# A hybrid decoder layer: twenty of 52 projection blocks as seven half-size products, and the mLSTM and attention steps beside the remaining ones

## The chip, the cores and the metric

One Trainium2 chip, one core. The metric is the device time of one execution in microseconds; lower is better. The kernel before takes 1984.62 us (median of three runs, 1983.13 to 1986.1).

## What is computed

One step of a decoder layer for a prompt of 1024 tokens and a group of 8 x 4 sample tokens that share all weights (1056 columns in all; D = 1024):

```python
h = LN0(x) * (1 + scale1) + shift1
z = h @ w_in + b_in        # mLSTM q, k (4 x 128), v, og (4 x 256), i, f; attention q (16 x 64), k, v (4 x 64); gm, ga (1024)
A = mlstm(q, k, v, i, f, state)              # 4 heads, chunks of 128, running max
B = window_attention(qa, ka, va, cache)      # 16 heads on 4 groups, window 128, sinks, ALiBi
merged = sigmoid(gm) * (A * sigmoid(og) @ w_bm) + sigmoid(ga) * (B @ w_ba)
x = LN1(alpha * x + gate1 * (merged @ w_out))
h2 = LN0(x) * (1 + scale2) + shift2
x = LN2(alpha * x + gate2 * (glu(conv3(h2 @ w_up)) @ w_down))
```

All in fp32; the outputs are both groups' rows and the new states (C, n, m, keys, values, convolution).

## The kernel before

An fp32 product is made of three products of parts: each operand is split into a high part (a cast to the reduced type, ScalarE) and a low part (operand minus high part, VectorE), and TensorE adds hi x hi, hi x lo and lo x hi in PSUM. The core's eight PSUM banks are L (three, for the projections), PD (two), PE, PF and PG (side work).

The projection `h @ w_in` goes in 52 blocks of 128 features and one of gate rows (`gate`, L1197 on). A block runs over three token tiles (384, 384, 288) and 8 chunks of D: 3 x 24 matmuls of `group` (L440 to L451). `evac_in` (L1170 on) takes each tile out of PSUM; ScalarE adds the bias or takes the tanh (L1180, L1184), VectorE scales (L1182). `Stream` (L393 on) loads a block's weights (L403), casts (L424) and subtracts (L428) a block or two ahead.

All else of this stage is *side work*, written as generators: `gate_rows` (L632 on: gates, two scans, exponentials), `mlstm(h)` for four heads (L753 on), `swa_pair` and `swa(g)` (L980 on, four attention groups). While the program is written, `pulse(us)` advances a clock by the products' time and takes a step of the first generator in the queue `sides` at `rate[0]` steps a microsecond:

```python
        if sides:
            clock[1] += us * rate[0]
            while clock[1] >= 1.0:
                clock[1] -= 1.0
                step_side()
```

So the order of every engine's instructions is fixed when the kernel is built; at run time each engine goes through its own list in order, and waits where an operand isn't there. The rates in this stage are 0.442, 0.395 and 0.35 (`RATES`, L34). SP issues nearly all DMAs, in one list. `later(us, fn)` puts an issue so many us of products further on. Before the last block `finish_sides()` takes all steps that are left, with no product between them.

An mLSTM head loads (first step) its decay row E (L757), the scaled query factor qA (L758), both spread over 128 partitions, and the old state C in two halves (L761); the second step makes E and the parts of q (L766 to L785); then a chunk of 128 tokens a step: scores and three transposes into bank PE (L799, L196), smT and the parts of v and of the weighted keys (L804 to L807), the products a step later (L789). At its end come the sample tokens, the new state (`new_state`, L906, L910, stored at L915), a norm and `hs`, transposed (L937), and the output rows go to DRAM (`hD`, L943). v and og of the head are still in SBUF from the projection. An attention step copies scores out of PD (L1142, L1143), adds biases, takes the exponentials (L1122), transposes, multiplies with v (L1092) and normalises; one step of a group also holds the sample tokens (L1039 to L1081).

Of the kernel before, what the change touches and what calls it, by code (L numbers as in the profile page):

```python
# [18 lines left out]
D = 1024  # L19
# [31 lines left out]
# columns of the table of constants  # L51
# [52 lines left out]
def hybrid_step(ctx: ExitStack, tc: tile.TileContext, I, O):  # L104
# [85 lines left out]
    # the rows of c in pieces of 128  # L190
# [7 lines left out]
    # vectors along the features, transposed: 0.. b_in (16 + 36 blocks), 52.. b_ada, 100.. norm_w,  # L198
    # 108.. b_down, 116.. b_up, 160.. conv_b, 204.. conv_w (3 x 44)
# [22 lines left out]
    def ada_load(ca, cb, f0, n=256):  # L222
        """Features f0 .. f0 + n of the factors ca and cb: their weights."""
# [43 lines left out]
    # silu(c), transposed  # L267
# [109 lines left out]
    def h_lo(k, ti, eng):  # L377
# [4 lines left out]
        h_f[k][1] += 1  # L382
        if h_f[k][1] == 3:
            drop(h_f.pop(k)[0])

# [1 line left out]
    class Stream:  # L387
        def __init__(self, specs):
            self.specs = specs
            self.raws, self.parts, self.loaded = {}, {}, 0  # L390

        def load(self, upto):
            while self.loaded <= min(upto, len(self.specs) - 1):  # L393
# [14 lines left out]
        def prep(self, i, later_lo=False):  # L408
            if i >= len(self.specs) or i in self.parts:
                return  # L410
# [43 lines left out]
    # ================= phase A: the combined projection, mLSTM, window attention =================  # L454
# [11 lines left out]
    for h in range(4):  # L466
        blk("k", h, 512 + 128 * h)
        blk("q", h, 128 * h)
        if h == 0:
            order.append(("gate", 0))  # L470
            specs.append(("gate",))
        blk("v", 2 * h, 1024 + 256 * h)
        blk("v", 2 * h + 1, 1024 + 256 * h + 128)
        blk("og", 2 * h, 2056 + 256 * h)
        blk("og", 2 * h + 1, 2056 + 256 * h + 128)
    gates = [("gm", j, 4616 + 128 * j) for j in range(8)] + [("ga", j, 5640 + 128 * j) for j in range(8)]
    gates = deque(gates)

    def add_gates(n):
        for _ in range(n):  # L480
            blk(*gates.popleft())
# [5 lines left out]
    blk("ka", 0, 4104)  # L487
    blk("va", 0, 4360)
    add_qa(0)
    add_gates(3)  # L490
    add_qa(1)
    add_gates(2)
    blk("ka", 1, 4104 + 128)
    blk("va", 1, 4360 + 128)
    add_qa(2)
    add_gates(4)
    add_qa(3)
    add_gates(7)

    # the order of all later products: branches, output product, feed-forward  # L500
# [25 lines left out]
    win = Stream(specs)  # L526

    # the first products take the chunks of h as they come
# [64 lines left out]
    # later constants  # L593
    v2, v3, v4 = slot(name="v2"), slot(name="v3"), slot(name="v4")
    rows(v2, 0, I["b_up"], 0, 44)
    rows(v2, 44, I["conv_b"], 0, 44)
    rows(v3, 0, I["conv_w"], 0, 88)
    rows(v4, 0, I["conv_w"], 88 * 128, 44)
# [7 lines left out]
    def late_consts():  # L606
        transpose(PF[:, 0:88], v2[:88, :128], 88)
# [105 lines left out]
    def cache_load(p):  # L713
        """The cached keys and values of a pair of groups."""
# [21 lines left out]
    def norm_tail(num, den, ecol, n):  # L736
        """The layer norm of num / max(|den|, e): its factor is (var(num) + eps max(|den|, e)^2)^-0.5."""
# [37 lines left out]
        # operands in two parts: q, v with a column of ones, the scores and the weighted keys  # L775
# [68 lines left out]
        # the state after the prompt  # L844
# [6 lines left out]
        # the sample group: all its tokens as one block  # L851
# [145 lines left out]
    def swa(g):  # L997
# [37 lines left out]
        def sample():  # L1035
            """The sample group: its rows are (sequence, head, token)."""
# [158 lines left out]
    def gate_rows_in(i):  # L1195
        """The gates' rows: products with both parts of the weights side by side, then their sum."""
# [47 lines left out]
    for h in range(4):  # L1244
        after["og", 2 * h + 1] = [lambda h=h: mlstm(h)]
    after["og", 7].append(state_n_out)
# [5 lines left out]
    def raw_pieces(src, ti):  # L1252
        """Loads a token tile of eight blocks that wait in DRAM."""
# [10 lines left out]
    def refill(raws, ti):  # L1264
        """Puts a token tile into the operand tiles, whose old contents its products have used."""
# [9 lines left out]
    rate[0] = RATES[0]  # L1275
# [611 lines left out]
```

## Time and profile before

| | |
|---|---|
| median of three runs | 1984.62 us |
| span of the profiled execution | 1981.8 us |
| TensorE busy | 1942.6 us, 98% |
| VectorE busy | 997.7 us, 50% |
| ScalarE busy | 723.3 us, 36% |
| GpSimd (POOL) busy | 308.9 us, 16% |
| mean DMA rate | 95 GB/s |

The profile is of one execution; its own time is known by its span, from the first to the last instruction, and the runs are timed apart. Busy times count the instructions on each engine; a matmul's end is modelled, so the distance from one start to the next says more than its length. "Idle before" names what ended the engine's wait. In the window views PEclk is the granted TensorE clock as a share of full speed.

### The profile page before, as it was taken

Reading aid. Unit: us, or ns where it says so; the run is one execution under the profiler, and the core shown is the slowest. Engines: PE = TensorE matmul, PEld = TensorE weight load, DVE = VectorE, ACT = ScalarE, POOL = GpSimd, SP = SyncE. Lnnn points to the kernel's source line nnn. Section 1 sums busy time; section 2 is a strip of 40 time slices with the busy share of each in tenths; the row PEclk is TensorE's granted clock in tenths of the full one; section 3 lists DMA queues with packets and bytes.
Section 4 is the critical chain, followed back from the end, with each engine's and each line's share of the span. In section 5 each row is a group of like instructions: output and inputs, shape, how many; then the busy total and the mean of one; then the engine's idle time right before and its main releaser. Section 6 shows DMA issues by size and latency. Waiting matters only on the chain. (4 is left out here: it accounts for less than half of the span.)

```text
span 1981.8 us, 31279 instructions
## 1 busy us (share of the span) xinstructions
PE 1942.6 (98%) x12597; PEld 1858.1 (94%) x12597; DVE 997.7 (50%) x2166; ACT 723.3 (36%) x1522; POOL 308.9 (16%) x592
## 2 busy tenths in 40 slices
PE   6999999999999999999999999999999999999996
PEld 4899999999998989999999999999999999999995
DVE  4454444444544535241454455564554554645579
ACT  4534334343546445331312454353131312222331
POOL 2013223231123131200000333100000000000007
PEclk9999999999999999999999999999999999999998
DMA  9151424324220322497524142111212020211533
GB/s 289 47 140 25 140 35 119 84 70 100 69 76 23 112 72 60 136 345 244 159 65 128 54 129 67 36 38 48 60 35 62 28 69 27 63 34 49 194 130 130
DMA packets 214362, 187.86 MB, mean 95 GB/s; under 512 B 8849, under 2 KB 197953, under 8 KB 214185
## 3 DMA queue, kind: packets, MB, share of 16 engines
q1 hardware_dynamic: 213437, 185.26, 31.1%
q8 instruction: 98, 1.61, 0.3%
q10 hardware_dynamic: 780, 0.61, 0.1%
q14 instruction: 47, 0.39, 0.1%
HBM read 150.06 MB, written 37.81 MB: 95 GB/s over the span
## 5 line engine op out<-in xcount | busy, mean ns | idle before, releaser
L450 PE MATMUL L<-hhi,whi 128*128 128x384 f32 (+1 forms) x1600 | 526.4, 329 | 0.1
L450 PE MATMUL L<-hlo,whi 128*128 128x384 f32 (+1 forms) x1600 | 517.0, 323 | 0.0
L450 PE MATMUL L<-hhi,wlo 128*128 128x384 f32 (+1 forms) x1600 | 516.5, 323 | 0.0
L450 PE MATMUL L<-mhi,whi 128*128 128x384 f32 (+1 forms) x1248 | 407.4, 326 | 4.9 <-DVE r L1466 3.0
L450 PE MATMUL L<-mhi,wlo 128*128 128x384 f32 (+1 forms) x1248 | 404.1, 324 | 0.4 <-DVE wlo L428 0.4
L450 PE MATMUL L<-mlo,whi 128*128 128x384 f32 (+1 forms) x1248 | 403.3, 323 | 0.0
L428 DVE TENSOR_TENSOR wlo<-wraw,whi 128x1024 fp32r<-128x1024 f32 (+1 forms) x148 | 174.5, 1180 | 331.3 <-ACT whi L424 330.8
L450 PEld LDWEIGHTS L<-hhi,whi 128*128 128x128 f32 x1600 | 301.5, 188 | 6.6 <-issue 4.8
L450 PEld LDWEIGHTS L<-hlo,whi 128*128 128x128 f32 x1600 | 301.9, 189 | 0.3
L450 PEld LDWEIGHTS L<-hhi,wlo 128*128 128x128 f32 x1600 | 301.4, 188 | 0.0
L450 PEld LDWEIGHTS L<-mhi,whi 128*128 128x128 f32 x1248 | 235.4, 189 | 6.7 <-DVE r L1466 3.3
L450 PEld LDWEIGHTS L<-mhi,wlo 128*128 128x128 f32 x1248 | 234.9, 188 | 1.0 <-DVE wlo L428 1.0
L450 PEld LDWEIGHTS L<-mlo,whi 128*128 128x128 f32 x1248 | 235.3, 189 | 0.1
L1511 ACT ACTIVATE u<-L,vT 128x384 f32<-128x384 f32 (+1 forms) x132 | 71.8, 545 | 378.6 <-PE L L450 378.6
L424 ACT CAST whi<-wraw 128x1024 fp32r<-128x1024 f32 (+1 forms) x148 | 149.2, 1009 | 28.3 <-DMA wraw<-in_w_up 25.3
L450 PE MATMUL L<-ahi,whi 128*128 128x384 f32 (+1 forms) x432 | 139.9, 324 | 0.0
L450 PE MATMUL L<-ahi,wlo 128*128 128x384 f32 (+1 forms) x432 | 139.4, 323 | 0.0
L450 PE MATMUL L<-alo,whi 128*128 128x384 f32 (+1 forms) x432 | 139.3, 323 | 0.0
L1524 DVE SCALAR_TENSOR_TENSOR y<-u,vT,y 128x1023 f32<-128x1023 f32 (+3 forms) x92 | 113.7, 1235 | 2.5
L1534 POOL COPY ucol<-u 128x2 f32<-128x2 f32 x44 | 10.3, 234 | 631.7 <-ACT u L1511 631.7
L1680 DVE TENSOR_TENSOR facc<-L,facc 128x384 f32<-128x384 f32 (+1 forms) x120 | 62.7, 522 | 58.6 <-PE L L450 58.4
L298 POOL TENSOR_SCALAR rstd<-mv 128x1 f32<-128x1 f32 (+1 forms) x36 | 22.0, 611 | 400.6 <-DVE mv L307 377.2
(422 smaller groups left out, 2652.4 us busy)
## 6 DMA issues: line engine op xcount, KB each, us to landing
wraw<-in_w_in SPq DMA_DIRECT2D x52, 512.0 KB
wada<-in_w_ada SPq DMA_DIRECT2D x44, 512.0 KB
wraw<-in_w_up SPq DMA_DIRECT2D x44, 512.0 KB
wraw<-in_w_down SPq DMA_DIRECT2D x24, 384.0 KB
hD<-og SPq DMA_DIRECT2D x8, 528.0 KB
gmD<-gm SPq DMA_DIRECT2D x8, 528.0 KB
haD<-ha SPq DMA_DIRECT2D x8, 528.0 KB
gaD<-ga SPq DMA_DIRECT2D x8, 528.0 KB
```

The lines of the kernel that those rows point to most:

```text
L298: G.tensor_scalar(r[:n], var, eps, None, op0=OP.add)
L424: A.copy(hi[:, :n], t[:, :n])
L428: V.tensor_tensor(lo[:, :n], t[:, :n], hi[:, :n].bitcast(F32), op=OP.subtract)
L450: T.matmul(ps[:, :nt], x[:, c], y[:, t0:t0 + nt], start=i == 0, stop=i == last)
L1511: A.activation(u[:, t0:t0 + n], ps[:, :n], AF.Identity, bias=b)
L1524: V.scalar_tensor_tensor(y[:, f:b], u[:, f - d:b - d], w[i], y[:, f:b], op0=OP.mult, op1=OP.add)
L1534: G.tensor_copy(aux["ucol"][:, c, 0:2], u[:, SEQ - 2:SEQ])
L1680: V.tensor_tensor(fx, ps[:, :nt], fx, op=OP.add)
```

## The change

Blocks gm4 to gm7, v0 to v7 and og0 to og7 (twenty) are now made in ten pairs. For a pair (256 features) h and the weights are cut in halves along D (even and odd chunks), features and tokens (two groups of 2 x 264), and Strassen's scheme in Winograd's form takes seven products of 4 chunks each for eight: per pair and token group 7 x 12 matmuls of 264 columns, 168 for a pair, where two blocks had 144 of 384 and 288 columns. The sums of h are made once (`tprep`), those of the weights for each pair on VectorE (`step`); a product's bank, one of all eight in a ring, is added to earlier ones by VectorE or copied by ScalarE. No side work runs meanwhile.

The order is now: gm0 to gm3 in the old way with `tprep` and the first pair's weights beside them at 0.68 steps a us; the ten pairs; the four overwritten halves of h are loaded again; then `gate` and 28 blocks in the old way, at 0.56 steps a us, with all mLSTM and attention steps beside them. The v and og blocks go to DRAM (`pD`) and are loaded in the first step of `mlstm(h)`, ahead of E, qA and C. `mlstm(h)` is queued after block q h.

```diff
-    for h in range(4):
         blk("k", h, 512 + 128 * h)
         blk("q", h, 128 * h)
-        if h == 0:
-            order.append(("gate", 0))
-            specs.append(("gate",))
-        blk("v", 2 * h, 1024 + 256 * h)
...
+    NG = 4
+    for j in range(NG):
+        blk("gm", j, 4616 + 128 * j)
+
+    PAIRS = [(kind, 2 * j, c0 + 256 * j) for kind, c0, js in (("gm", 4616, range(NG // 2, 4)), ("v", 1024, range(4)),
+                                                              ("og", 2056, range(4))) for j in js]
...
+    order.append(("gate", 0))
+    specs.append(("gate",))
+    add_kq(0)
+    add_fill(1)
+    add_kq(1)
+    add_fill(1)
+    add_kq(2)
+    add_fill(1)
+    add_kq(3)
+    add_kva(0)
     add_qa(0)
...
     def mlstm(h):
-        qT, kT, vT0, vT1, og0, og1 = proj["q", h], proj["k", h], proj["v", 2 * h], proj["v", 2 * h + 1], \
-            proj["og", 2 * h], proj["og", 2 * h + 1]
+        qT, kT = proj["q", h], proj["k", h]
+        vT0, vT1, og0, og1 = (slot(name=k) for k in ("v", "v", "og", "og"))
+        for t, key in ((vT0, ("v", 2 * h)), (vT1, ("v", 2 * h + 1)), (og0, ("og", 2 * h)), (og1, ("og", 2 * h + 1))):
+            S.dma_start(t, pD[key])
         E, qA = slot(name="E"), slot(name="qA")
...
+        def step(self, i):
+            if i == 0:
+                self.sums = [slot(name="fsum") for _ in range(2)]
+                self.sum(1, self.q(1, 0), self.q(1, 1), OP.add)
+                self.sum(3, self.q(0, 0), self.q(1, 0), OP.subtract)
+            elif i == 1:
+                self.sum(2, self.s(1), self.q(0, 0), OP.subtract)
+                self.sum(4, self.q(0, 1), self.s(2), OP.subtract)
+                self.pa = self.parts(self.raw[0])
...
+        def product(self, p, g):
+            ps = ring[0][:, :HT]
+            ring.rotate(-1)
+            for kp in range(4):
+                (wh, wl), (xh, xl) = self.weights(p, kp), operand(p, kp, g)
+                for i, (x, y) in enumerate(((wh, xh), (wh, xl), (wl, xh))):
+                    T.matmul(ps, x, y, start=kp == 0 and i == 0, stop=kp == 3 and i == 2)
...
+            if p == 1:
+                A.copy(u1, ps)
+            elif p == 2:
+                self.put(0, g, 0, ps, u1)
+            elif p == 6:
+                V.tensor_tensor(u2, ps, u1, op=OP.add)
+            elif p == 7:
+                V.tensor_tensor(u3, ps, u2, op=OP.add)
+            elif p == 4:
+                self.put(1, g, 0, ps, u3)
+            elif p == 5:
+                V.tensor_tensor(u5, ps, u2, op=OP.add)
+                self.put(1, g, 1, ps, u3)
+            elif p == 3:
+                self.put(0, g, 1, ps, u5)
...
+    rate[0] = 0.68
+    sides.append(first_pair())
+    for i in range(NG):
+        if i == NG - 2:
+            pairs[0].load()
+        direct(i)
+        if i == NG - 1:
+            finish_sides()
...
+    fast(pairs, at_end)
+    drop(hf[0], hf[2], *t3s, *b12)
+    late_loads()
+    rate[0] = 0.56
+    for i in range(NG, len(order)):
+        direct(i)
```

(`put` is one VectorE operation of 264 columns that adds bank, bias and the other term into the finished block.)

**SP, from the end of one mLSTM head to the loads of the next (head 0 to head 1); vD and ogD are the new DRAM copies.** Before:

```order
58 L915 DMA out_s_C<-C0_98_1289 128x8x128
59 L915 DMA out_s_C<-C0_99_1290 128x8x128
60 L403 DMA wraw_126_2129<-in_w_in 128x8x128
61 L943 DMA hD0_689<-og_88_1109 128x1056
62 L943 DMA hD1_690<-og_92_1206 128x1056
63 L403 DMA wraw_130_2216<-in_w_in 128x8x128
64 L757 DMA E_131_2233<-mD_683 128x1056
65 L758 DMA qA_132_2234<-aD_684 128x1056
66 L761 DMA C0_133_2237<-in_state_mlstm_C 128x8x128
67 L761 DMA C0_134_2238<-in_state_mlstm_C 128x8x128
```

and in the changed kernel:

```order
114 L932 DMA out_s_C<-C0_246_3547 128x8x128
115 L932 DMA out_s_C<-C0_247_3548 128x8x128
116 L772 DMA v_268_4272<-vD2_1921 128x1056
117 L772 DMA v_269_4273<-vD3_1863 128x1056
118 L772 DMA og_270_4274<-ogD2_2789 128x1056
119 L772 DMA og_271_4275<-ogD3_2729 128x1056
120 L774 DMA E_272_4280<-mD_675 128x1056
121 L775 DMA qA_273_4281<-aD_676 128x1056
122 L778 DMA C0_274_4284<-in_state_mlstm_C 128x8x128
123 L778 DMA C0_275_4285<-in_state_mlstm_C 128x8x128
124 L960 DMA hD0_681<-og_242_3537 128x1056
125 L960 DMA hD1_682<-og_243_3538 128x1056
```

The loads of E and qA (L757, L758 before; L774, L775 now) stood behind the old head's output rows and a weight load; now they stand behind both stores of the old head's C, directly, and behind four loads of v and og.

**TensorE, at the last block of the projection.** Before, with the block ahead of it and its own first rows:

```order
4738 L450 MATMUL L1_72<-hhi_55_588,whi_369_8386 128x288
4739 L450 MATMUL L1_72<-hlo_56_589,whi_369_8386 128x288
4740 L450 MATMUL L1_72<-hhi_55_588,wlo_370_8387 128x288
4741 L450 MATMUL L2_73<-hhi_29_262,whi_373_8494 128x384
4742 L450 MATMUL L2_73<-hlo_30_263,whi_373_8494 128x384
4743 L450 MATMUL L2_73<-hhi_29_262,wlo_374_8495 128x384
```

and now (PD takes scores, PG and PE transposes, PF the products with v; in place of the dots more of the same kinds):

```order
4899 L447 MATMUL L1_72<-hhi_55_588,wlo_437_8527 128x288
4900 L1154 MATMUL PD0_74<-khi_443_8687,q2_445_8706 128x256
...
4908 L196 MATMUL PG_78<-cst_83,ss_8786 128x128
4909 L196 MATMUL PG_78<-cst_83,ss_8786 32x128
4910 L196 MATMUL PE_76<-cst_83,scr_450_8753 128x128 x4
4911 L1154 MATMUL PD0_74<-khi_443_8687,q2_445_8706 128x256
...
4919 L1090 MATMUL PG_78<-pnT_8928,vs1_7888 64x64 x2
...
4980 L1109 MATMUL PF_77<-scr_454_8757,vn_410_7887 64x256
4981 L447 MATMUL L2_73<-hhi_29_262,whi_440_8678 128x384
4982 L447 MATMUL L2_73<-hlo_30_263,whi_440_8678 128x384
```

Before, one block follows on the other. Now 81 rows of attention (4900 to 4980, twelve steps of the last group) stand between them with no product of a block among them.

## Rows read from the trace of the kernel before

**Rows 1.** The page: busy us of an engine (share of the span) xinstructions.

```profile
PE 1942.6 (98%) x12597; PEld 1858.1 (94%) x12597; DVE 997.7 (50%) x2166; ACT 723.3 (36%) x1522; POOL 308.9 (16%) x592
```

**Rows 2.** Waits of PE in the whole run: us in total, times, longest us.

```profile
PE PE L196 <- DMA v<-in_b_down: 4.9, 1, 4.9
```

**Rows 3.** Window 60 to 760: us, busy us by engine, PEclk, DMA share, GB/s.

```profile
60.00:760.00 700.00, 699.87 (x4719) 665.13 (x4717) 328.22 (x1012) 312.24 (x800) 163.00 (x300) 1.00 0.30 80
```

**Rows 4.** Timeline of PE: start us, us, operation; tiles of 288 and 384 columns.

```profile
910.12 0.29 PE L450 MATMUL L<-hhi,whi 128*128 128x288 f32 x1
...
913.29 0.34 PE L450 MATMUL L<-hhi,whi 128*128 128x384 f32 x1
913.47 0.34 PE L450 MATMUL L<-hlo,whi 128*128 128x384 f32 x1
```

**Rows 5.** The same, an mLSTM product of 258 columns.

```profile
329.06 0.28 PE L789 MATMUL PD<-CTh,qh 128*128 128x258 f32 x1
329.18 0.29 PE L789 MATMUL PD<-CTl,qh 128*128 128x258 f32 x1
```

**Rows 6.** Groups by line and shape, VectorE: busy us, mean ns, idle before.

```profile
L428 DVE TENSOR_TENSOR wlo<-wraw,whi 128x1024 fp32r<-128x1024 f32 x124 | 151.6, 1223 | 278.1 <-ACT whi L424 277.6 <-DMA wraw<-in_w_in 0.5
...
L1271 DVE TENSOR_TENSOR hlo<-raw,hhi 128x384 fp32r<-128x384 f32 x32 | 15.3, 551 | 0.1
```

**Rows 7.** Timelines of PE, DVE and ACT, the start of head 1.

```profile
224.38 1.65 DVE L766 TENSOR_SCALAR E<-E,colQ 128x128 f32<-128x128 f32 x8
...
227.53 1.03 ACT L777 CAST qh<-qA 128x1024 fp32r<-128x1024 f32 x1
...
231.39 0.37 ACT L807 ACTIVATE wx<-PE,colQ 128x128 fp32r<-128x128 f32 x1
...
229.98 0.38 PE L799 MATMUL PE<-q,k 128*128 128x128 f32 x2
```

**Rows 8.** Timelines of PE and ACT, the gates' chain.

```profile
80.54 1.96 PE L1210 MATMUL L<-gpart,cst 32*36 32x384 f32 x6
...
108.90 1.08 ACT L694 ACTIVATE gr<-gr 4x1056 f32<-4x1056 f32 x1
...
110.07 0.74 PE L196 MATMUL PD<-cst,gr 128*128 128x128 f32 x5
```

**Rows 9.** Timeline of SP's DMA queue: issue us, us; heads 0 and 1.

```profile
112.35 9.43 SPq L403 DMA_DIRECT2D wraw<-in_w_in  x2
...
209.75 1.40 SPq L757 DMA_DIRECT2D E<-mD  x1
```

**Rows 10.** Window in which those transfers run (columns as rows 3).

```profile
212.00:216.00 4.00, 4.00 (x25) 4.00 (x24) 1.33 (x2) 0.58 (x1) 0.00 (x0) 1.00 1.07 337
```

**Rows 11.** Timelines of PE and DVE, the end of head 0.

```profile
201.04 0.73 PE L906 MATMUL PD<-wskM,wv 96*128 96x512 f32 x2
...
201.58 2.16 DVE L910 SCALAR_TENSOR_TENSOR C<-C,decb,PD 128x128 f32<-128x128 f32 x8 [2.05 <-PE PD L906]
...
207.24 0.31 PE L196 MATMUL PG<-cst,hs 32*128 32x32 f32 x2
```

**Rows 12.** Timeline of ACT, the copies of three attention steps.

```profile
682.37 0.85 ACT L1142 COPY scr<-PD 128x256 f32<-128x256 f32 x2 [0.57 <-PE PD L1137]
...
688.96 0.62 ACT L1142 COPY scr<-PD 128x256 f32<-128x256 f32 x2
...
692.06 0.61 ACT L1142 COPY scr<-PD 128x256 f32<-128x256 f32 x2
```

**Rows 13.** Windows behind 16 narrow matmuls at 511.36 (columns as rows 3).

```profile
513.00:514.00 1.00, 1.00 (x5) 0.97 (x5) 0.97 (x9) 0.27 (x1) 0.00 (x0) 0.61 1.04 313
514.00:516.00 2.00, 2.00 (x8) 2.00 (x8) 0.08 (x1) 0.43 (x1) 0.00 (x0) 0.50 0.03 8
```

**Rows 14.** Windows in the start (columns as rows 3).

```profile
14.00:20.00 6.00, 1.17 (x6) 0.47 (x4) 2.85 (x6) 1.81 (x2) 1.58 (x6) 1.00 1.06 353
20.00:26.00 6.00, 5.62 (x31) 2.29 (x30) 0.00 (x0) 1.90 (x2) 0.68 (x2) 1.00 1.10 348
```

More of the change, by code (lines that the diff above doesn't have):

```diff
@@ L464, in blk, with add_fill, add_kq @@
         specs.append(spec_in(c0))
[L466 removed]
+    NG = 4
[3 more added lines that the diff above has]
+                                                              ("og", 2056, range(4))) for j in js]
+    fill = deque(range(8))
+    def add_fill(n):
+        for _ in range(n):
+            j = fill.popleft()
+            blk("ga", j, 5640 + 128 * j)
+    def add_kq(h):
         blk("k", h, 512 + 128 * h)
         blk("q", h, 128 * h)
[L469 to L481 removed]
     def add_qa(g):
@@ new lines, in t1_split, with operand @@
+    def t1_split():
+        for kp in range(4):
+            hi, lo = (quarters(t)[:, :, 1, :] for t in acts[2 * kp])
+            x = quarters(hf[2 * kp])[:, :, 0, :]
+            A.copy(hi, x)
+            V.tensor_tensor(lo, x, hi.bitcast(F32), op=OP.subtract)
+        drop(hf[4], hf[6])
+    def operand(p, kp, g):
+        e, o = 2 * kp, 2 * kp + 1
+        if p in (1, 2, 3, 5):
+            k, half_ = {1: (e, 0), 2: (o, 0), 3: (o, 1), 5: (e, 1)}[p]
+            return tuple(quarters(t)[:, g, half_, :] for t in acts[k])
+        if p == 7:
+            return tuple(t[:, g, :] for t in t3_ops[kp])
+        return tuple(quarters(t)[:, g, 0 if p == 4 else 1, :] for t in t_ops[kp])
@@ new lines, in fast @@
+    def fast(pairs, at_end):
+        prev = None
+        t1_split()
+        for n, pr in enumerate([*pairs, None]):
+            nxt = pairs[n + 1] if n + 1 < len(pairs) else None
+            for pos, p in enumerate((1, 3, 6, 2, 7, 4, 5)):
+                who = prev if p == 3 else pr
+                if who is not None:
+                    for g in range(2):
+                        who.product(p, g)
+                if p == 3 and prev is not None:
+                    drop(*prev.ps[1])
+                if pr is None:
+                    if pos == 1:
+                        return
+                    continue
+                if pos == 0:
+                    if n:
+                        pr.step(2)
+                elif pos == 1:
+                    pr.step(3)
+                    pr.step(4)
+                elif pos == 2 and nxt is not None:
+                    nxt.load()
+                elif pos == 3:
+                    drop(*pr.pa)
+                elif pos == 4 and nxt is not None:
+                    nxt.step(0)
+                elif pos == 5:
+                    drop(pr.pq)
+                    if nxt is not None:
+                        nxt.step(1)
+                elif pos == 6:
+                    drop(*pr.ps[0])
+                if nxt is None:
+                    at_end(pos)
+            prev = pr
@@ new lines, in hybrid_step, with finisher, finish, out @@
+    pD = {}
+    def finisher(kind, idx):
+        def finish(blk_, z):
+            j = idx + blk_
+            if kind != "v":
+                A.activation(z, z, AF.Tanh, scale=0.5)
+                f = hnw[:, j:j + 1] if kind == "og" else 0.5
+                V.tensor_scalar(z, z, f, f, op0=OP.mult, op1=OP.add)
+            t = dram.tile([128, TOK], F32, name=f"{kind}D{j}")
+            (gD if kind == "gm" else pD)[kind, j] = t
+            def out():
+                S.dma_start(t, z)
+                drop(z)
+            later(2.0, out)
+        return finish
@@ L1277, in hybrid_step, with direct @@
+    pairs = []
+    for kind, idx, c0 in PAIRS:
+        base = {"v": VB_V, "og": VB_OG, "gm": VB_GM}[kind] + idx
+        pairs.append(Pair((WIN, DIN, c0), finisher(kind, idx), [vT[:, base + i:base + i + 1] for i in range(2)]))
+    def direct(i):
+        kind, idx = order[i]
         last = i == len(order) - 1
-        if (kind, idx) == ("k", 1):
-            rate[0] = RATES[1]
-        if (kind, idx) == ("ka", 0):
-            rate[0] = RATES[2]
         if last:
```

157 lines of the change are left out of this document (134 added, 23 removed).

## The prediction, made before the changed kernel was run

> **What bounds the kernel now.** I read the page first: TensorE is busy for 1942.6 of the 1981.8 us [rows 1]. Then the table of its waits: the longest is 4.9 us, in the start [rows 2]. Then a window: in the 700 us from 60 to 760, where all mLSTM and attention lies, it is busy for 699.87 us at a granted clock of 1.00 [rows 3]. So every product taken away there is worth its pitch, and every wait that is put there is lost in full. The order of the instructions is fixed per engine, so a product cannot step in for one that waits.
>
> The sum stands against the profiled execution, span 1981.8 us; the median of the runs, 1984.6, is 2.8 above it, and I add that at the end. About 0.2% (4 us) can be told from no change.
>
> **1. The seven-product pairs.** In the timeline a tile of 384 columns goes at 0.175 us a matmul and one of 288 at 0.132 (24 of them from 910.12 to 913.29) [rows 4]. A block is 48 x 0.175 + 24 x 0.132 = 11.58 us, ten pairs 231.6. The new products have 264 columns; the nearest row is 258 columns at 0.12 (329.06, 329.18) [rows 5], the line through 288 and 384 gives 0.121, and I take 0.1213. Ten pairs x 168 matmuls = 203.8 us: **-27.8**. By the Trainium skill's page "TensorE: Matmul & The Clock Gate", section "Back-to-back issue gap", an isolated matmul takes its columns at 2.4 GHz and a few ns, which would make 264 columns about 0.1125 us (an estimate from that page) and the saving 43; the same rule gives 0.1225 where the row of 288 columns shows 0.132, so the row decides, and the rule gets no chance of its own: its 15 us would not change the sign.
>
> Can VectorE follow? Per pair: 14 additions of 264 columns out of PSUM at about 0.43 (0.551 for 384), 6.0 us; three low parts of 1024 at 1.22 and one of 512 at about half, 4.3; four sums of 512 at about 0.7, 2.7; the scaling of finished blocks 1.6 [rows 6]. That is 14.6 of the pair's 20.4 us; ScalarE has three casts of some 1.03 [rows 7] and little else. Eight banks in a ring give seven products of slack. I cost it at nothing.
>
> **2. Start of the pairs.** Beside the four direct gm blocks (46.3 us, of which four tiles of 384, 16.8, are done before as early products: 29.5) VectorE now makes the sums of h and the first pair's parts, some 31 us of operations that the nearest row of that size (1.22, [rows 6]) prices, each 0.6 to 1.3; some wait for the copies to DRAM and for ScalarE's casts. Bounds 2 and 10, I take **+5**.
>
> **3. End of the pairs.** The four overwritten halves of h come back from DRAM and are split again (four casts, four subtractions, about 0.55 each) before the gates' products. 1 to 4, I take **+2**.
>
> **4. The gates.** The gates' rows end on TensorE at 80.54 + 1.96 = 82.5; the chain over VectorE's scans, ScalarE's exponentials and two table loads ends at 109.98, and the transposes that need it start at 110.07, at once [rows 8]. It takes 27.4 us. In the new order only 120 matmuls of k and q lie between the two, 80 at 0.175 and 40 at 0.132: 19.3 us. Full difference 8; a part of the chain is VectorE's own weights (two subtractions). 3 to 9, **+6**.
>
> **5. Heads.** An mLSTM head now loads v and og (4 x 528 KB) ahead of E and qA, and SP issues in order. In before its queue had nothing ahead: E was issued at 209.75, 20 us before the first products at 229.98 [rows 7, 9]. The transfers run at 337 GB/s with all DMA engines busy [rows 10], E's arithmetic begins at 224.38, and bank PE is free again when wx has been read, at 231.39 + 0.37: 7.4 us after E has landed [rows 7]. In the changed order (the two pieces of SP's order above) the loads of heads 1 to 3 stand behind both stores of the old head's C, which need the last state update, 2.16 us of VectorE that ended 2.7 after its products [rows 11]. From those products, TensorE's order has 24 matmuls, two transposes, then 39 matmuls to the first chunk and 9 to the second: 13.8 us with the wait of step 6. The bytes: stores 1.0 MB, v and og 2.1, E 0.5, 3.7 MB in all at 337 GB/s = 11, so E lands at 2.7 + 11 = 14 and the bank is free at 21: 7 us late, 4 to 10; I take 6 each, **+18**. Head 0 stands behind the two cache copies of 992 KB, whose successor waited 9.4 us for its issue already in before [rows 9], and behind a wraw: 2 + 0.5 + 2.1 + 0.5 MB = 15 us plus 2 to 4 to land, against 12.2 us of products. The bank is free at 26 where the next chunk stands at 12: 14; 6 to 18, and as the gates' wait (step 4) gives the queue a start I take **+10**.
>
> **6. The heads' ends.** The last products of a head's state start at 201.04, the transposes of hs, which wait for a norm over VectorE, POOL and ScalarE, at 207.24 [rows 11], some 0.3 us after it is there. At 0.56 steps a us only 24 matmuls (3.9 us) lie between, against 5.4 to 6: 1.5 x 4, 2 to 8, **+4**.
>
> **7. Attention.** A group's step goes from copies to copies in 3.10 us on ScalarE (688.96 to 692.06); with the sample step it is 6.59 (682.37 to 688.96) [rows 12]. The new TensorE period of a step is 1/0.56 = 1.8 us of products and about 2.5 of its own, 4.3: longer than 3.10, so an ordinary step costs nothing. Behind a sample step 6.6 + 3.1 stands against 8.6, and a group's start waits for ScalarE's casts and VectorE's (1.03 and 1.22 for the like, [rows 6, 7]): 3 a group, 4 to 20 for all, **+8**.
>
> **8. The rest before the last block.** The denser rate does not suffice: 12 steps of the last group are issued bare between two blocks (the order of TensorE above; before none). Five hold scores, 5 x 3.1 = 15.5; the sample's wait adds 3; seven end-steps at some 1.8 (POOL's norm, a copy, the transposes) 12: about 31 us, of which the products are 15. 10 to 22, **+14**.
>
> Sum: -27.8 + 5 + 2 + 6 + 18 + 10 + 4 + 8 + 14 = +39, so 2021 of span and **2024** as a run. The lower bounds (heads 1 to 3: 12, head 0: 6) give +12, 1997, the upper ones (30 and 18) +93, 2078. I stay in the lower half of each bound because a stall lets the other engines run ahead for the next.
>
> **Rivals.**
> *The clock.* Rows first: where 16 narrow matmuls ran for 2 us, the granted clock went to 0.61 and 0.50 for the next 3 us [rows 13], the lower of TensorE's two levels, 1.2 GHz: some 1.5 us lost. But from 14 to 20 TensorE was busy for 1.17 us in all, and the products of the 6 us after it show 1.00 [rows 14], which speaks against. If six of the stalls above are each followed by one such stretch, 6 x 1.5 = +9: 2033. The Trainium skill's page "TensorE: Matmul & The Clock Gate", section "HAM oscillation — how this bites in real kernels", says that gaps in which TensorE waits for a transfer bring it to half clock and that the next products run cold; this rule speaks against the change, and the row agrees as to level and length though not as to what brings it on.
>
> *The loads keep ahead* (ends faster). If SP issues a head's loads 20 us before the chunk needs them, as in before [rows 7, 9], steps 5 to 7 fall away: -27.8 + 5 + 2 + 3 + 10 = -8, 1977. It is decided by one place, whether the stores of C hold the queue: under 7 us from the last state update to E's landing would do. The order of SP speaks against it, and the bytes.
>
> *Only part stalls.* Heads at 2 each, attention at nothing: -27.8 + 5 + 2 + 6 + 8 + 4 + 14 = +11, 1996. Same mechanism as the forecast, at its low end.
>
> *VectorE binds the pairs.* If additions out of PSUM with rearranged halves cost half as much again and its order makes the products wait, a pair takes 24 us in place of 20.4: +36 on the forecast, 2060. For it: the fullest engine after TensorE there; against: 6 us of room and the ring.
>
> **Chances.** Forecast 0.50 (own range 2005 to 2045), clock 0.12, only part 0.14, loads ahead 0.16, VectorE 0.08. Faster by over 0.2%: the loads-ahead case, 0.16 less a little that ends near zero, 0.14. Same 0.05. Slower 0.81. The range reaches from 1974, so that it takes in the loads-ahead case, to 2056; out are VectorE binding and the ends of the others.
>
> **What would show it.** Right: about 168 matmuls of 264 columns in 20.4 us a pair; waits of TensorE on bank PE released by VectorE's smT and ScalarE's copies at the second chunk of every head, 5 to 14 us; a wait on gr after the gates; half-idle TensorE for 15 us before the last block; 1942 us of busy time down by 28. Wrong: if TensorE's waits between the pairs and the last block sum to under 28 us, steps 5 to 8 are overpriced and the kernel is faster; if a pair takes over 21 us, step 1 fails.

## The result, and the profile after

The changed kernel takes 2110.34 us (median of four runs, 2109.16 to 2111.52), the kernel before 1984.19 beside it: a ratio of 1.0631 with a 95% interval of 1.0616 to 1.0646, 126 us slower. The direction was forecast, the size was not: 2024 with a range up to 2056. The profiled execution has a span of 2109.4 us, 127.6 more than before.

The page's engine row, which answers to [rows 1]:

```profile
PE 1968.8 (93%) x12837; PEld 1863.6 (88%) x12837; DVE 1116.5 (53%) x2374; ACT 738.0 (35%) x1530; POOL 300.5 (14%) x592
```

TensorE is busy 26 us longer, although it has 26 us less to do (34 of these 52 us are the lower clock, below), and stands for another 100. The windows show where. The kernel is cut at four places on TensorE: the gates' first product, the first product of the last projection block, the first of the branch products behind it, and the seventeenth block of these. The kernel before (columns as in rows 3: length, busy us and counts by engine, granted clock, DMA share, GB/s):

```profile
0.00:72.80 72.80, 55.04 (x395) 41.74 (x395) 35.89 (x97) 36.96 (x64) 13.47 (x40) 1.00 0.74 221
72.80:841.70 768.90, 768.77 (x5193) 727.71 (x5191) 359.16 (x1143) 344.59 (x918) 179.62 (x320) 1.00 0.30 82
...
853.20:1065.90 212.70, 212.70 (x1442) 200.23 (x1441) 84.86 (x163) 44.47 (x83) 0.00 (x0) 1.00 0.57 182
1065.90:1966.60 900.70, 894.60 (x5503) 876.94 (x5501) 498.50 (x736) 287.77 (x439) 106.80 (x225) 1.00 0.23 72
```

and the changed kernel, in which the first window holds the ten pairs:

```profile
0.00:313.50 313.50, 288.01 (x2218) 273.09 (x2218) 195.16 (x369) 105.77 (x159) 13.57 (x40) 0.98 0.43 130
313.50:950.30 636.80, 554.73 (x3606) 498.00 (x3606) 317.70 (x1080) 289.17 (x832) 172.07 (x320) 0.94 0.30 85
...
962.00:1187.00 225.00, 216.31 (x1442) 200.88 (x1442) 87.83 (x168) 47.82 (x89) 0.00 (x0) 0.98 0.59 189
1187.00:2094.50 907.50, 898.10 (x5503) 879.94 (x5501) 498.83 (x736) 287.77 (x439) 105.86 (x225) 0.99 0.23 71
```

Up to the last block the first two windows are 841.7 us before and 950.3 now, +108.6; the window of the branch products is 12.3 longer and the rest 6.8. In the second window of the kernel before TensorE is never idle, at clock 1.00; now it is idle for 82 of 636.8 us and the clock is 0.94 in the mean. That window can be priced: before it held 49 blocks, now 27 with the same side work, and a block is 11.58 us, so without any loss it would take 768.9 - 22 x 11.58 = 514 us. **123 us are lost there.** "Lost" below is always this number, with the blocks that the kernel in question has, and this window is "the stage".

The waits of TensorE over the whole run (us in total, times, longest); before, the longest of all was 4.9 us, in the start [rows 2], and none of these eight kinds was over 0.5 us:

```profile
PE PE L816 <- DVE wx L827: 27.1, 5, 9.0
PE PF L1109 <- POOL scr L1120: 15.5, 11, 2.7
PE PE L240 <- DMA wada<-in_w_ada: 13.7, 5, 8.3
PE PD L1154 <- DVE scr L1160: 8.8, 5, 2.6
PE PD L1154 <- DVE q L1034: 7.8, 10, 1.2
PE PE L196 <- DMA v<-vD: 7.7, 2, 6.8
PE PG L196 <- ACT hs L766: 5.5, 4, 1.9
PE PD L196 <- ACT gr L709: 5.4, 1, 5.4
```

The first is the heads' second chunk (bank PE); the second, fourth and fifth are attention (11.5 us of the second and 3.5 of the fourth lie behind 905 us, where steps stand bare); the last three are v on its way back from DRAM, the heads' ends and the gates. The prediction had a term for each of these places. It did not name two of the waits: v itself, for which TensorE stands 6.8 us at head 0 (step 5 looked at E alone), and the weights of the adaLN factors (the third row, here mostly behind the last block, 8.3 us).

The pairs themselves, in TensorE's timeline, with the two waits at their start, and then the last pair:

```profile
100.92 0.59 PE L1419 MATMUL PF<-hhi,fhi 128*128 128x264 f32 x1 [4.44 <-ACT fhi L1377]
...
104.82 0.59 PE L1419 MATMUL PF<-hhi,flo 128*128 128x264 f32 x1 [3.09 <-DVE flo L1378]
105.21 0.42 PE L1419 MATMUL PF<-hhi,fhi 128*128 128x264 f32 x1
105.43 0.42 PE L1419 MATMUL PF<-hlo,fhi 128*128 128x264 f32 x1
...
307.21 0.29 PE L1419 MATMUL PF<-hhi,fhi 128*128 128x264 f32 x1
307.34 0.28 PE L1419 MATMUL PF<-hlo,fhi 128*128 128x264 f32 x1
```

A matmul of 264 columns goes at 0.12 us as priced, and at 0.22 right behind the waits.

A head's start (head 1 to head 2), SP's queue:

```profile
502.55 4.22 SPq L932 DMA_DIRECT2D out_s_C<-C  x2
506.88 1.70 SPq L772 DMA_DIRECT2D v<-vD  x2
...
509.63 0.63 SPq L774 DMA_DIRECT2D E<-mD  x1
```

and TensorE and VectorE there:

```profile
503.69 0.73 PE L923 MATMUL PD<-wskM,wv 96*128 96x512 f32 x2
...
518.33 1.66 DVE L783 TENSOR_SCALAR E<-E,colQ 128x128 f32<-128x128 f32 x8 [6.71 <-DMA E<-mD]
...
526.99 0.80 PE L816 MATMUL PE<-q,k 128*128 128x128 f32 x2 [8.99 <-DVE wx L827]
```

From the last state products at 503.69 to the second chunk at 526.99 it is 23.3 us; step 5 had 21 for the bank against 13.8 of products. E arrives at 518.33, 8.7 us after its issue, because both stores of C and four loads of v and og go before it. What was not priced is the clock in the same place:

```profile
520.00:525.00 5.00, 0.00 (x0) 0.00 (x0) 3.89 (x10) 3.55 (x5) 1.32 (x2) 0.82 1.16 329
525.00:530.00 5.00, 3.01 (x13) 3.02 (x14) 2.06 (x7) 1.65 (x6) 0.77 (x2) 0.50 1.04 345
530.00:535.00 5.00, 5.00 (x35) 5.00 (x34) 2.59 (x9) 2.45 (x8) 2.81 (x7) 1.00 0.24 64
```

In the window that contains the wait's end TensorE runs at 0.50, in the next it is back. By the trace's records of the granted clock, the changed kernel has 75 us at the lower level in the stage of 636.8 us (that is the 0.94), TensorE busy for 56 of them, so that 28 us of products are lost; over the whole run 39, against 5 before.

### The profile page after: what moved, and what is told of

The parts are those of the page before. It is cut to its first block, busy times and chain, and to the rows that moved or that the text cites. A ratio compares the mean times of both kernels' runs of the same rounds, so it can differ in the third digit from the quotient of the medians.

```text
span 2109.4 us, 32157 instructions
## 1 busy us (share of the span) xinstructions
PE 1968.8 (93%) x12837; PEld 1863.6 (88%) x12837; DVE 1116.5 (53%) x2374; ACT 738.0 (35%) x1530; POOL 300.5 (14%) x592
## 5 line engine op out<-in xcount | busy, mean ns | idle before, releaser
L447 PE MATMUL L<-hhi,whi 128*128 128x384 f32 (+1 forms) x1120 | 375.7, 335 | 0.4 <-ACT k L1201 0.3
L447 PE MATMUL L<-hlo,whi 128*128 128x384 f32 (+1 forms) x1120 | 366.3, 327 | 0.0
L447 PE MATMUL L<-hhi,wlo 128*128 128x384 f32 (+1 forms) x1120 | 366.0, 327 | 0.0
L425 DVE TENSOR_TENSOR wlo<-wraw,whi 128x1024 fp32r<-128x1024 f32 (+1 forms) x128 | 150.8, 1179 | 314.4 <-ACT whi L421 309.6
L447 PEld LDWEIGHTS L<-hhi,whi 128*128 128x128 f32 x1120 | 215.6, 192 | 7.2 <-issue 4.8
L447 PEld LDWEIGHTS L<-hlo,whi 128*128 128x128 f32 x1120 | 215.8, 193 | 0.3
L447 PEld LDWEIGHTS L<-hhi,wlo 128*128 128x128 f32 x1120 | 214.7, 192 | 0.0
L421 ACT CAST whi<-wraw 128x1024 fp32r<-128x1024 f32 (+1 forms) x128 | 128.5, 1005 | 28.6 <-DMA wraw<-in_w_up 25.1
L447 PEld LDWEIGHTS L<-alo,whi 128*128 128x128 f32 x432 | 81.2, 188 | 0.0
```

Source lines behind the costliest of these rows:

```text
L421: A.copy(hi[:, :n], t[:, :n])
L425: V.tensor_tensor(lo[:, :n], t[:, :n], hi[:, :n].bitcast(F32), op=OP.subtract)
L447: T.matmul(ps[:, :nt], x[:, c], y[:, t0:t0 + nt], start=i == 0, stop=i == last)
```

## The experiments

Each was run once, beside the kernel before (1983 to 1987 us). Windows are cut at the same four places. All in one table, the changed kernel first:

| run | us | blocks in the stage | lost in it, us |
|---|---|---|---|
| changed kernel | 2110 | 27 | 123 |
| e1 E ahead of v | 2092 | 27 | 105 |
| e2 fill blocks late | 2095 | 27 | 112 |
| e3 packing alone | 2106 | 27 | 120 |
| e4 twenty blocks more | 2254 | 47 | 41 |
| e5 two waits filled | 2109 | 27 | 122 |
| e6 loads a head ahead | 2080 | 27 | 91 |
| e7 e2 and e6 | 2062 | 27 | 78 |
| e8 e4 and e6 | 2223 | 47 | 7 |
| e9 e7, late store | 2047 | 27 | 73 |
| e10 e9, six pairs | 2030 | 35 | 42 |
| e11 e9, two pairs | 2024 | 43 | 31 |
| e12 ScalarE copies | 2101 | 27 | 114 |

**e1, E ahead of v.** In `mlstm`, the loop that loads v and og is put behind the two loads of E and qA:

```diff
+        S.dma_start(E, dap(mD, h * TOK, [[0, 128], [1, TOK]]))
+        S.dma_start(qA, dap(aD, h * TOK, [[0, 128], [1, TOK]]))
         for t, key in ((vT0, ("v", 2 * h)), (vT1, ("v", 2 * h + 1)), (og0, ("og", 2 * h)), (og1, ("og", 2 * h + 1))):
             S.dma_start(t, pD[key])
-        S.dma_start(E, dap(mD, h * TOK, [[0, 128], [1, TOK]]))
-        S.dma_start(qA, dap(aD, h * TOK, [[0, 128], [1, TOK]]))
```

> A head's first step issues E and qA ahead of v and og; nothing else changes. If the reload of v and og in front of E is what holds the heads (queue theory), E lands some 6 us sooner, the 27 us of TensorE's waits on bank PE behind wx shrink to about 10, and the run takes 2095 to 2103 us; the wait for v (7.7 us) grows by at most 3 us a head. If the heads are late because the engines' chains from one step to the next are longer than the products between them (packing theory), it stays at 2107 to 2112.

2091.95 us, 18 less; lost 105. Its waits of TensorE:

```profile
PE PE L196 <- DMA v<-vD: 15.0, 6, 10.4
...
PE PE L816 <- DVE wx L827: 5.5, 6, 2.2
```

The waits behind wx fall from 27.1 to 5.5, those for v rise from 7.7 to 15.0 (10.4 of it at one place, head 0). The queue theory holds, and the gain is larger than it said: the waits behind wx fall to 5.5 us where 10 were expected, and what the lower clock costs in the stage falls from 28.2 to 25.7 us.

**e2, fill blocks late.** Five ga blocks, not two, behind the last qa; three places between earlier blocks give theirs up (the expectation says two).

```diff
-    add_fill(1)
     add_kq(3)
...
-    add_fill(1)
     add_kva(1)
...
     add_qa(2)
-    add_fill(1)
     add_qa(3)
-    add_fill(2)
+    add_fill(5)
```

> Two ga blocks are moved from among the earlier blocks to the end (five ga blocks follow the last qa, two did), so that 1 to 2 steps and not 12 stand bare before the last block; rate and all else as in the changed kernel. Tail theory: the 25 us lost between 905 and 950 and most of the 12 us lost behind the last block (loads of h that could not be issued ahead) go: 2075 to 2090. Rival (the loss only moves forward, since the same steps then wait elsewhere): 2100 to 2112.

2095.02 us, 15 less, lost 112; between the two theories. Only 11 of the tail's 23 us are gained in the stage: the tail's steps now stand beside blocks and still wait there, and the branch window stays at 223.6 (e9 shows why). So about half of what these steps cost hangs on the bare place.

**e3, the packing alone.** The twenty blocks are made by `direct`, first, without side work; `tprep` and `fast` are gone; v and og go to `pD` as in the changed kernel.

```diff
+    for j in range(4, 8):
+        blk("gm", j, 4616 + 128 * j)
+    for j in range(8):
+        blk("v", j, 1024 + 128 * j)
+    for j in range(8):
+        blk("og", j, 2056 + 128 * j)
...
-    fast(pairs, at_end)
```

> The twenty blocks are made in the old way, first and with no side work beside them; v and og still go to DRAM and come back, the rest of the order and the rate 0.56 stay. The sums of h and of the weights are gone. If the seven-product pairs by themselves do what was forecast (they took 212 us with 6 us of start, where twenty old blocks take 231.6, and 6 us of waits lie around them), this takes 2118 to 2128 us, and the whole slowing lies in the packing. If the pairs cost elsewhere (VectorE's work, the reload of h, the clock behind them), it takes 2090 to 2110.

2106.40 us. Its windows:

```profile
0.00:327.00 327.00, 309.25 (x1978) 296.14 (x1979) 81.85 (x166) 94.19 (x152) 13.53 (x40) 1.00 0.41 121
327.00:961.30 634.30, 556.58 (x3608) 500.18 (x3605) 314.51 (x1074) 289.27 (x830) 170.46 (x320) 0.94 0.31 90
...
973.00:1185.70 212.70, 212.70 (x1443) 200.00 (x1442) 84.87 (x163) 44.54 (x83) 0.00 (x0) 1.00 0.58 182
```

To the gates it takes 327.0 us where the changed kernel takes 313.5: at their place the pairs gain 13.5 (25.8 less of products, 12 of waits, clock and split around them). The next window is as long as with the pairs, 634 against 637, lost 120. So **the order alone, with the way over DRAM, makes the kernel 122 us slower**, and the pairs by themselves give 13.5. That the two totals are only 4 apart lies behind the last block: 212.7 here as in the kernel before, 225.0 with the pairs. By its total the run stands where the rival put it (2090 to 2110), that the pairs cost elsewhere, and my 2118 to 2128 missed that. The 12 us behind the last block are the order on SP, though, and not the pairs' own work: here the store that e9 moves is issued at 964.79, behind the first 16 loads for the branch products (926.29), and in the changed kernel ahead of them.

**e4, twenty blocks more as cover**, with ga's weights once more, into a buffer that nothing reads; rate 0.36.

```diff
+    def add_dup(n):
+        for _ in range(n):
+            blk("xx", len(order), 5640 + 128 * (len(order) % 8))
...
-    rate[0] = 0.56
+    rate[0] = 0.36
```

> As the changed kernel, with twenty blocks more (products with the weights of ga again, copied out by ScalarE into a buffer that is given back; nothing reads them) spread over the stage with mLSTM and attention, and the rate at 0.36 in place of 0.56. They add 231.6 us of products. Packing theory: the 129 us lost in this stage fall to 15 to 30 (the gates and head 0 remain in part), 2225 to 2255. Queue theory (reload of v and og): the heads' 45 to 60 us remain, 2265 to 2290. If the losses belong to the steps as such: 2330 to 2342.

2253.99 us, at the edge of the packing theory. The stage:

```profile
313.60:1100.20 786.60, 762.37 (x5046) 717.77 (x5046) 341.74 (x1100) 336.32 (x912) 168.92 (x320) 0.97 0.29 82
```

With 47 blocks it would be 745.7 without loss: 41 lost, more than the 15 to 30 expected. 82 of 123 us come back with products to lie beside (and the lower rate that spreads the steps over them), though the same steps and the same loads are there. What is left stands at the heads (16.5 us behind wx).

**e5, two waits filled** with 24 products each, ahead of the first pair and of the gates' transposes.

```diff
+    def warm_up(n):
+        ps = lbank()
+        for i in range(n):
+            T.matmul(ps[:, :384], acts[1][0][:, :128], acts[3][0][:, :384], start=i == 0, stop=i == n - 1)
...
+    warm_up(24)
     fast(pairs, at_end)
```

> Two waits of TensorE in the changed kernel are filled with 24 products of 384 columns each (4.2 us, of operands that are there; nothing reads them): the 4.4 us ahead of the first pair's products and the 5.4 us ahead of the gates' transposes. Clock theory (the granted clock halves because TensorE stood idle before): the first pair's products run at 0.12 us a matmul and not at 0.22, no half-clock stretch follows at 100, and the one at 349 shrinks; 3 to 6 us less in all, 2104 to 2107. Rival (the clock falls for another reason, the wait itself is all that is lost): the stretches stay, 2109 to 2112.

2108.81 us, 1.5 less: inside the rival's range, and by the time alone not to be told from no change (the four runs of the changed kernel begin at 2109.16). But the windows at the gates show what sets the clock off. The changed kernel:

```profile
345.00:350.00 5.00, 0.37 (x3) 0.05 (x1) 4.90 (x15) 2.72 (x4) 0.00 (x0) 0.91 0.40 108
350.00:355.00 5.00, 4.21 (x19) 4.15 (x20) 1.36 (x4) 1.32 (x2) 0.00 (x0) 0.50 0.72 112
```

and with the wait filled:

```profile
345.00:350.00 5.00, 4.53 (x26) 4.21 (x24) 4.90 (x14) 2.79 (x4) 0.00 (x0) 1.00 0.40 108
350.00:355.00 5.00, 4.27 (x33) 4.07 (x34) 1.74 (x7) 1.26 (x2) 0.00 (x0) 1.00 0.66 112
```

The products behind the filled wait run at 1.00, with nothing else changed there. At the pairs the filled wait was only the first of two; the second (3.4 us, for the low part of the weights) was still there, and the half clock came behind it. So at these two places the clock theory holds for what sets it off. The gain was too small because the next waits took it back: those for v grow from 7.7 to 9.4 us and those behind wx from 27.1 to 28.6, and from 366, within the first of them, the clock is at the lower level for 20.5 us, where it was for 17. This agrees with the rule of the Trainium skill's page "TensorE: Matmul & The Clock Gate", section "HAM oscillation — how this bites in real kernels", that gaps between bursts of products bring the clock down.

**e6, loads a head ahead.** Step 5 of a head issues E, qA, v and og of the next; head 0's v and og go ahead of the gates, the two copies of the cache ahead of the pairs.

```diff
+            if s == 5 and h < 3:
+                rows_load(h + 1)
+                vog_load(h + 1)
             yield
         drop(qh, ql, vx, wx)
```

> Loads of E, qA, v and og of a head are issued in step 5 of the head before it (head 0: v and og ahead of the gates), and the two copies of the cache are issued before the pairs; all else as in the changed kernel. Queue theory: no head waits for a transfer, the waits on bank PE behind wx and for v fall under 5 us in all, with the clock behind them: 2060 to 2078. Packing theory (the chain of a head's start is too long for the products between, whenever the loads come): 2084 to 2092, as with E ahead of v alone.

2080.16 us, 30 less than the changed kernel, lost 91; two us above what the queue theory said, with the waits behind wx at 8.2 and none for v. So the late loads (v, og, E, qA and, ahead of head 0, the cache copies) cost 32 us of the 123, and the packing the rest. The clock does not follow as the queue theory had it: what it costs falls from 13 to 4 us up to the heads' end and grows from 15 to 23 in the attention behind, 27 in all where it was 28.

**e7, both repairs** (e2 and e6).

> Both repairs at once, loads a head ahead and more ga blocks at the end. If they are two independent losses the gains add: the former's less 13 to 17, 2045 to 2063. If what is gained at the heads is lost again in the attention groups, which then start no earlier relative to TensorE: 2065 to 2080.

2062.49 us, lost 78: 31.5 and 11 by themselves, 44.5 together. These two losses add, within 2 us.

**e8, cover and loads ahead** (e4 and e6).

> Twenty blocks more in the stage (rate 0.36), and the loads a head ahead. The 44 us that were still lost with the twenty blocks alone (2254) fall to 10 to 20, 2220 to 2232, if density and the queue together are all of it; if something else holds (the gates' chain, the clock by itself), 2240 to 2254.

2222.80 us. The stage:

```profile
314.30:1066.70 752.40, 748.80 (x5047) 706.27 (x5047) 341.70 (x1100) 336.24 (x912) 170.40 (x320) 0.99 0.30 83
```

745.7 would be without loss: 7 us are left of 123, the clock is at 0.99. Density and the queue together are all of it. Here the same narrow products of the attention run as in the changed kernel, and the clock holds, but for two stretches of 10 us in all. Both the waits are gone and the narrow products lie farther apart, so for the attention this run doesn't tell which of the two brings the clock down.

**e9, SP's queue at the end.** e7, with the store of the last attention group's rows put 20 us of products later.

```diff
-        later(4.0, out)
+        later(24.0 if g == 3 else 4.0, out)
```

In the changed kernel SP stood at this store until the last attention step was done (35.8 us, the longest of its waits there, first row), and the first 16 loads for the branch products, which don't need it, came behind it, and then the adaLN weights:

```profile
SPq L1178 <- DVE ha L1113: 50.3, 2, 35.8
...
950.80 0.90 SPq L1178 DMA_DIRECT2D haD<-ha  x2
951.80 10.04 SPq L1277 DMA_DIRECT2D raw<-hD  x16
...
970.18 11.29 SPq L230 DMA_DIRECT2D wada<-in_w_ada  x8
...
978.26 1.06 PE L240 MATMUL PE<-wada,cT 128*32 128x256 f32 x2 [8.27 <-DMA wada<-in_w_ada]
```

> Both repairs (loads a head ahead, ga blocks late), and the store of the last attention group's rows is issued 20 us of products later, so that SP issues the loads of the mLSTM's rows for the branch products before it and not behind it. If this store held the queue at the end (the loads were issued 10 us after the last block could have begun, and the branch products then waited 8 us for the adaLN weights queued behind them), the stretch of the sixteen blocks behind the last block falls from 223 to 213 us, as in the kernel before: 2050 to 2055. If the wait lies in the transfers themselves, 2060 to 2064.

2047.02 us, 15.5 less than e7, more than expected (the kernel before took 1987.13 beside it and 1983.96 beside e7, so the gain is not smaller than that):

```profile
314.60:901.40 586.80, 544.11 (x3606) 488.48 (x3606) 318.24 (x1080) 289.09 (x832) 171.72 (x320) 0.97 0.31 94
913.10:1125.50 212.40, 212.40 (x1442) 199.85 (x1441) 85.17 (x163) 44.23 (x83) 0.00 (x0) 1.00 0.58 185
```

The branch window is at 212.4, as before. The queue theory holds; the stage ends 5 us sooner too.

**e10 and e11, six pairs and two pairs**, from e9: og, and then v as well, are made in the old way beside the heads. 36 and 44 blocks carry the side work, rates 0.46 and 0.44.

```diff
-    PAIRS = [(kind, 2 * j, c0 + 256 * j) for kind, c0, js in (("gm", 4616, range(NG // 2, 4)), ("v", 1024, range(4)),
-                                                              ("og", 2056, range(4))) for j in js]
+    PAIRS = [(kind, 2 * j, c0 + 256 * j) for kind, c0, js in (("gm", 4616, range(NG // 2, 4)),("v", 1024, range(4))) for j in js]
```

> The former with six pairs (gm4 to gm7, v) in place of ten; og is made in the old way beside each head, so the side work has 36 blocks to lie beside, rate 0.46. Four pairs fewer give back 10 us of products. Density theory: the 80 us still lost beside 28 blocks and the 10 us beside 48 lie on a falling curve, 25 to 52 here: 2015 to 2037. If what is left is lost at fixed places (starts of heads and groups), 2060 or more.

> The former with two pairs (gm4 to gm7), v and og both made beside the heads, 44 blocks for the side work, rate 0.44. Eight pairs fewer than ten give back 20.6 us. Density theory: 15 to 30 us lost, 2002 to 2023; the kernel before stays ahead, since two pairs save 5 us and their start costs 7 to 10. If what is left is lost at fixed places: 2070.

2029.85 and 2024.38 us. Their stages:

```profile
231.40:880.20 648.80, 628.66 (x4185) 579.40 (x4182) 335.07 (x1109) 306.90 (x860) 174.84 (x320) 0.97 0.29 81
```

```profile
152.30:882.90 730.60, 709.91 (x4759) 661.64 (x4759) 347.17 (x1120) 330.22 (x896) 182.10 (x320) 0.99 0.28 76
```

Without loss they would be 606.8 and 699.4: 42 and 31 lost, where ten pairs lose 73. More cover, less loss, as density has it, and every pair given up costs 2.6. e11 missed its range by a us; that its rate of 0.44 was still high may be why, and wasn't tried. In e10 the branch window is 217.9 us in spite of the late store, in e11 212.4. No count of pairs tried comes within 37 us of the kernel before, and none was found that beats it.

**e12, a shorter circle in the attention step** (a circle is a chain of waits over several engines that closes on itself from step to step). What the prediction took for a full step's time was 3.10 us [rows 12]. ScalarE's copies of the scores in the changed kernel:

```profile
773.25 0.63 ACT L1159 COPY scr<-PD 128x256 f32<-128x256 f32 x2
775.92 0.27 ACT L1113 COPY ha<-PF 128x128 f32<-128x128 f32 x1 [2.04 <-DVE ha L1113]
...
778.21 0.63 ACT L1159 COPY scr<-PD 128x256 f32<-128x256 f32 x2
```

Full steps lie 4.96 us apart, and ScalarE stands for 2.04 of them behind VectorE's half of the copy out of PF, which is in VectorE's list behind the reductions of the step before. e12 lets ScalarE copy both halves:

```diff
-                    (A.copy if j else V.tensor_copy)(ha[j][:, n * 128:(n + 1) * 128], PF[:, j * 128:(j + 1) * 128])
+                    A.copy(ha[j][:, n * 128:(n + 1) * 128], PF[:, j * 128:(j + 1) * 128])
```

> The changed kernel with one word changed in the attention step: both halves of the product with v are copied out of bank PF by ScalarE, where VectorE took one. In the trace of the changed kernel ScalarE stands 1.6 to 2.0 us in every full step, until VectorE's copy of its half is done, which stands in VectorE's list behind the four reductions of the step before; so a full step lasts 4.96 us (copies at 773.25 and 778.21), longer than TensorE's 4.3. Chain theory (this closed circle over ScalarE and VectorE sets the attention's pace): the step falls under 4.3, the 40 us lost between 655 and 905 fall to 12 to 22 and the tail's 23 by some: 2075 to 2095. Rival (GpSimd's masks and norm or the bank PD set it): 2105 to 2112.

2101.24 us, 9 less, lost 114:

```profile
773.00 0.62 ACT L1159 COPY scr<-PD 128x256 f32<-128x256 f32 x2
774.87 0.43 ACT L1113 COPY ha<-PF 128x128 f32<-128x128 f32 x2 [1.25 <-PE PF L1109]
...
777.64 0.62 ACT L1159 COPY scr<-PD 128x256 f32<-128x256 f32 x2
```

The step falls to 4.64, and what ScalarE waits for there is now TensorE, whose own full steps run without a wait there and take 4.65 and 4.26 us (its products with v start at 769.07, 773.72 and 777.98). So the circle set the pace, but only by some 0.3 us: TensorE's waits behind GpSimd's masks (PF, scr) fall from 15.5 to 7.5 us, which is nearly all of the gain. The chain theory is right on the place and wrong on the size. As long as before are the waits at the groups' starts (on PD for q, 7.8 us) and behind the sample steps (on PD for scr, 8.8), and the clock, 28 us in the stage.

## Why the prediction was right on the sign and wrong on the size

The forecast was +39 us of span and 127.6 came. Two terms failed above all: step 7, attention, which the sum had at 8 and the runs show at 40, and the clock, which the sum had at nothing and which costs 39 us over the run, against 5 before (28 of them lie in the stage, inside the places of steps 4 to 8). The queue was right in kind and too small.

The split of the 123 us by place prices every product at its mean distance in the kernel before: about 27 between 345 and 400 (gates and head 0), 37 to 655 (heads), 40 to 905 (attention), 23 to 950 (the bare steps); they sum to 127, within 4 of the window's number. The clock's 28 us are in them.

- **Step 1** (-27.8): the products are 25.8 us less. Right; VectorE kept up: behind the pairs' start no wait of TensorE among them stands in the table.
- **Steps 2 and 3** (5 and 2): waits of 4.4 and 3.1 at the first pair, 3 us of half clock behind them, 1.6 at the end. 12 for 7, inside the bounds.
- **Step 4** (6): a wait of 5.4. Right, and 3 us of half clock behind it that stand in the clock's account.
- **Steps 5 and 6** (28 and 4): the mechanism is right (order in SP's queue, E's landing, bank PE; e1 and e6), but for the wait for v itself. The waits of 27.1, 7.7 and 5.5 us make 40 where 32 were forecast. With the gates the places up to 655 show 64 for 38: the clock's 13 us and waits too short for the list came on top.
- **Step 7** (8, bounds 4 to 20): 40. The groups' starts and the sample steps, which it priced, take 13 us of waits. "So an ordinary step costs nothing" failed: the 3.10 us were read from a group's first steps, which hold no transposes and no product with v, and a full step takes 4.96 on ScalarE; TensorE waits 4.0 us for it before 905, and more in the bare steps (e12: 9 us over the stage). The clock takes 13 more, and the rest, some 8 us, is pauses too short for the list.
- **Step 8** (14): 23 and, unforeseen, +12 in the branch products, since SP stood at a store (e9). The 6.8 us in the rest of the run had no term either, and no run was made to explain them.
- **The clock** failed as a rival, and by a misread row. Six stalls at 1.5 us were priced, and the row of the start [rows 14], with 1.00 behind a long stand of TensorE, was held against them. But the trace's records of the granted clock begin at 25.1 us; where there is none the view prints 1.00. The products themselves show the lower level until then:

```profile
20.94 5.48 PE L240 MATMUL PE<-wada,cT 128*32 128x256 f32 x30 [0.38 <-DMA wada<-in_w_ada]
...
27.94 3.98 PE L240 MATMUL PE<-wada,cT 128*32 128x256 f32 x32 [0.43 <-DVE modT L263]
```

Of the first group two start every 0.43 us up to 24.8, and every 0.22 from 25.2 on, as the second group does. So the start never spoke against the clock. In the changed kernel 14 stretches at half clock begin between 99 and 990 us, and over the run the clock costs 34 us more than before. e5 shows for one wait that it is the wait that brings the stretch; for the attention that is not shown.
- **"I stay in the lower half of each bound because a stall lets the other engines run ahead"** went the wrong way: the losses of e2 and e6 add (e7), and many of the waits bring a second loss with them. But the upper bounds alone give 2078, still 32 short, which is about the clock: with it the sum comes near 2110, in part by luck, since step 7 was over its upper bound too. The sign was no luck: e3 shows the whole slowing in the order and the way over DRAM, and e8 that products beside the steps and early loads take nearly all of it away.

## What to carry to other kernels

Products that are taken out of a stage also were the cover of all that lay beside them: here the gain is 2.6 us a pair of blocks, and the loss of cover with the changed queue came to 12. Count the steps per us of products that a stage will have, and compare it with the longest full step's circle over all engines, read from a step that holds every part; here that circle was only 9 us of the 123, so price the starts of heads and groups by themselves. Where one engine's order is fixed, a wait costs itself and can cost the clock behind it as well. A store that waits in an in-order queue holds every load behind it. And before a granted clock of 1.00 is used as evidence, look at the distance between the products' starts in the same window.

## What the runs showed of the hardware that was not expected

In the changed kernel the granted clock fell to the lower of its two levels 14 times between 99 and 990 us: eight times in or behind waits of TensorE of 4.2 to 9.0 us (the pairs' start, the gates, the heads, the adaLN weights), six times behind waits of 0.5 to 2.2 us, five of these among the narrow products of the attention. In the stage of the kernel before it fell twice without any wait, once behind the narrow matmuls of [rows 13]. Products of 264 columns ran at 0.22 us in place of 0.12 meanwhile. A wait of 5.4 us that was filled with products that nothing reads was not followed by it: 1.00 in place of 0.50. So a wait's cost can go on after its end: of the 123 us lost in the stage 28 went to the lower level, 13 of them at the gates and heads. What brings it on in the attention, the short waits or the narrow products themselves, stays open.

Between 13.8 and 24.8 us the kernel before ran at the lower level too, by the distance between its products (transposes of 128 columns 0.21 us apart, and 0.11 from 26.5 on), though the window view shows 1.00 there: it has no record to show.
